# Low parts of every second up-projection weight tile by an accumulating transfer

## The chip, the cores and the metric

The kernel runs on one core of one Trainium2 chip. The metric is device time in microseconds (us) of one execution; smaller is better. A core has TensorE for matrix products (PE in the profile; PEld are its weight loads), VectorE (DVE), ScalarE (ACT), GpSimd (POOL) and SyncE (SP). Transfers from device memory (HBM) into the on-chip buffers (SBUF) are issued by SP and POOL, each in its own queue, and carried out by 16 DMA engines. Matrix products are summed up in PSUM.

## The reference, cut

Two layers over 256 tokens of width 2048, all in float32:

```
h    = rmsnorm(x) ; proj = h @ w_in[l]            # 2048 x 6144: q, k, v, gate_b, gate_c, conv_in
attn = differential attention (8 heads) of q, k, v
conv = gate_b * causal_conv3(gate_c * conv_in)
x    = x + concat([attn, conv]) @ w_out[l]        # 2048 x 2048
hm   = rmsnorm(x) @ w_up[l]                       # 2048 x 8192: the up-projection
x    = x + square(relu(hm)) @ w_down[l]           # 8192 x 2048: the down-projection
```

## The kernel before, in words

**Two parts for every operand.** To keep float32 accuracy on TensorE, each weight and each activation is split in two: a high part, which is the value rounded to the type float32r, and a low part, the value minus the high part. A product is then three products: high x high, high x low, low x high (`TERMS`, L35).

**Weight tiles.** All weights come through one stream of 768 tiles of 128 x 1024 values (512 KB), in the fixed order of the list `plan` (L269 to L285). Tiles of `w_in` for q, k, v, of `w_out` and of `w_down` cover 2 row blocks x 512 columns (`straight`); tiles of the gates, the convolution and `w_up` cover 4 row blocks x 256 columns (`turned`). `load_weights` (L288) lets SP load the next tile into one of `RAW` = 4 raw buffers. `split_weights` (L298) makes the parts: ACT copies the raw tile, rounding, into a high tile `whi` (L307), and DVE subtracts it from the raw tile into a low tile `wlo` (L308). `whi` and `wlo` have 3 buffers each (the pool `wpool`, L108). `weights` (L313) is called when TensorE's program comes to tile i; it sees to it that tiles up to i + `AHEAD` = i + 2 have been split ahead of it in program order. A buffer comes free when its last reader is done: a raw buffer after the subtraction, a high or low buffer after the matmuls that use it.

**The products.** `linear` (L322; q, k, v, w_out and down) takes a tile in 12 matmuls, three for each row block and half of the tokens. `linear_t` (L341; gates, convolution and up) holds the weights still and first runs the eight matmuls of a tile with its high part (512 columns: high and low activations side by side), then the eight with its low part (256 columns). Four tiles fill one accumulator of an up-projection step; `hidden` (L585) then takes it out of PSUM with ACT (copy of one half, relu, square, high part) and DVE (sum of the halves, low part). In each layer the MLP runs in four groups: one up stage of 8 accumulators (32 tiles), then one down stage of 32 tiles. So there are 256 up tiles. The index of a tile in `plan` decides below what is done with it; the four tiles of an up accumulator are even, odd, even, odd.

**Order.** TensorE's order is the program's own (`manual_schedule`, L115). Side work such as normalization, transposes and attention is put between the products in small pieces (`Background`, L52). The instructions of the other engines and queues are ordered by the framework's planner before the run; each engine then works through its list in order and waits where an operand isn't ready or a buffer isn't free. POOL issues transfers only for constants and tables near the start; in the MLP it has nothing to do.

**Other buffers.** `nat` (7 buffers of the tag `wide`, L109) holds intermediate 128 x 512 tiles: of `joined` and `hidden`, of the normalizations and of attention. `tmp` (3 buffers, L110) holds the scores of a head, `s`, in attention.

Of the kernel before, what the change touches and what calls it, by code (L numbers as in the profile page):

```python
# [9 lines left out]
F32 = mybir.dt.float32  # L10
F32R = mybir.dt.float32r
AF = mybir.ActivationFunctionType
ALU = mybir.AluOpType
AX = mybir.AxisListType

P = 128
# [7 lines left out]
DFF = 4 * D  # L24
# [4 lines left out]
CH = 512  # L29
WC = 256  # L30
KG = 4
RAW = 4
AHEAD = 2

TERMS = ((0, 0), (0, 1), (1, 0))  # L35
REL = 2 * S - P - 1
# [62 lines left out]
def trunk(ctx: ExitStack, tc: tile.TileContext, x, w_in, w_out, conv_w, q_norm_g, k_norm_g,  # L99
          lambda_q1, lambda_k1, lambda_q2, lambda_k2, subln_g, attn_norm_g, mlp_norm_g,  # L100
          w_up, w_down, rel_bias, selector, out):
    nc = tc.nc
# [2 lines left out]
    xpool = ctx.enter_context(tc.tile_pool(name="xpool", bufs=1))  # L105
    apool = ctx.enter_context(tc.tile_pool(name="apool", bufs=4))
    bpool = ctx.enter_context(tc.tile_pool(name="bpool", bufs=8))
    wpool = ctx.enter_context(tc.tile_pool(name="wpool", bufs=3))  # L108
    nat = ctx.enter_context(tc.tile_pool(name="nat", bufs=7))  # L109
    tmp = ctx.enter_context(tc.tile_pool(name="tmp", bufs=3))  # L110
    small = ctx.enter_context(tc.tile_pool(name="small", bufs=4))
    dram = ctx.enter_context(tc.tile_pool(name="dram", bufs=1, space=bass.MemoryType.DRAM))
    mm = ctx.enter_context(tc.tile_pool(name="mm", bufs=2, space=PSUM))
# [155 lines left out]
    plan = []  # L269
# [16 lines left out]
    loaded, parts_of = [], []  # L286

    def load_weights():  # L288
        i = len(loaded)
        if i < len(plan):  # L290
            w, row, c, nk = plan[i]
            cols = 2 * CH // nk
            raw = wpool.tile([P, nk, cols], F32, tag="raw", name=f"raw{i}", bufs=RAW)
            nc.sync.dma_start(
                raw, w[row:row + nk * P, c:c + cols].rearrange("(k p) c -> p k c", p=P))
            loaded.append(raw)

    def split_weights():  # L298
        i = len(parts_of)
        if i < len(plan):  # L300
            while len(loaded) <= i:
                load_weights()
            nk = plan[i][3]
            hi = wpool.tile([P, nk, 2 * CH // nk], F32R, tag="hi", name=f"whi{i}")
            lo = wpool.tile([P, nk, 2 * CH // nk], F32R, tag="lo", name=f"wlo{i}")
            for c in (slice(0, 1), slice(1, nk)) if i < 2 else (slice(0, nk),):
                nc.scalar.activation(hi[:, c], loaded[i][:, c], AF.Copy)  # L307
                nc.vector.tensor_sub(lo[:, c], loaded[i][:, c], hi[:, c].bitcast(F32))  # L308
            parts_of.append((hi, lo))

    used = [0]
# [1 line left out]
    def weights(w, row, c):  # L313

        i = used[0]
        used[0] += 1
        assert plan[i][1:3] == (row, c)
        while len(parts_of) < min(len(plan), i + 1 + AHEAD):
            split_weights()
        return parts_of[i]  # L320
# [45 lines left out]
    def joined(acc, name):  # L366

        low = nat.tile([P, 2, S], F32, tag="wide", name=f"{name}l")
        nc.scalar.activation(low, acc[:, :, 1], AF.Copy)
        whole = nat.tile([P, 2, S], F32, tag="wide", name=f"{name}w")  # L370
        nc.vector.tensor_add(whole, acc[:, :, 0], low)
        return whole
# [230 lines left out]
    for l in range(DEPTH):  # L603
# [3 lines left out]
        for half in range(2):  # L607
            h0 = 4 * half
            c0 = half * CH
# [16 lines left out]
        for q in range(AW // WC):  # L626
# [4 lines left out]
            i = joined(acc, f"ci{l}{q}")  # L631
# [66 lines left out]
```

## Time and profile before

| what | value |
|---|---|
| median of 3 runs | 2208.05 us (2205.59 to 2208.78) |
| the profiled execution: its own time | 2209.4 us |
| its span in the profile | 2207.6 us |
| mean granted TensorE clock | 0.999 |
| DMA packets and bytes | 302698, 410.99 MB, mean 186 GB/s |
| SP's queue, share of the 16 DMA engines | 61.0% |
| POOL's queue, share of the 16 DMA engines | 0.3% |
| read from HBM over the span | 406.96 MB |

How to read it. The profile is of one execution. In the engine rows a number in us is busy time, in brackets its share of the span, and x the count of instructions. A wait row reads: who waited, on which line, for whom, then us in total, times, the longest. A group row reads: line, engine, operation, output <- inputs with their shapes, count, then busy us and mean ns of one, then the idle time just before and what ended it. A timeline row starts with start and duration in us, a row of the chain as well. A row of the stretches table gives, for one stretch of the span, its length, each engine's busy time and count, the granted clock, the mean busy share of the DMA engines and GB/s. Issue rows end with the median us from a transfer's issue to its landing; where three numbers stand, they are the least, the median and the most.

### The profile page before, as it was taken

The page shows a single profiled execution, that of the slowest core. Times are in us where ns is not written, and L with a number is a line of the kernel's source. Part 1 is how long each engine was busy: PE and PEld are TensorE (multiplying, and loading weights), DVE is VectorE, ACT ScalarE, POOL GpSimd, SP SyncE. Part 2 cuts the span into 40 slices and gives each one's busy share as a digit, 9 for nine tenths or more (in the row PEclk, how much of TensorE's full clock was granted, in tenths as well). Part 3 has the DMA queues.
Part 4 walks back from the last instruction along what each step waited for, and adds up shares of the span by engine and source line. Part 5 has one row for each costly group of instructions (what it writes and reads, how often), then busy time and mean ns, then how long its engine had stood idle before and what let it go on. Part 6 is the DMA issues. An engine that isn't in the chain of part 4 may idle for free.

```text
span 2207.6 us, 28973 instructions
## 1 busy us (share of the span) xinstructions
PE 2193.6 (99%) x11242; PEld 1863.1 (84%) x11242; DVE 1257.4 (57%) x1561; ACT 1105.3 (50%) x1492; POOL 100.3 (5%) x120
## 2 busy tenths in 40 slices
PE   8999999999999999999999999999999999999999
PEld 6888888888888888888888888888888888888887
DVE  5577655555555555555556776555555555555554
ACT  6456445554454454355445664445534544544543
POOL 3021100000000000000011211000000000000000
PEclk9999999999999999999999999999999999999999
DMA  7554666666666666666666546666666666666665
GB/s 250 172 158 148 191 183 189 187 187 191 197 186 188 199 187 186 194 194 184 186 185 179 156 153 187 186 185 189 188 191 196 187 190 197 185 189 199 186 197 162
DMA packets 302698, 410.99 MB, mean 186 GB/s; under 512 B 12931, under 2 KB 193749, under 8 KB 302560
## 3 DMA queue, kind: packets, MB, share of 16 engines
q1 hardware_dynamic: 301520, 406.90, 61.0%
q0 software_dynamic: 992, 2.22, 0.3%
q8 instruction: 88, 1.44, 0.3%
q14 instruction: 50, 0.41, 0.1%
q10 hardware_dynamic: 48, 0.02, 0.0%
HBM read 406.96 MB, written 2.12 MB: 185 GB/s over the span
## 4 chain that ended last, share of the span: by engine, by line
PE 99%; DMA 0%; POOL 0%; DVE 0%; ACT 0%; issue 0%; SPq 0%; DVEq 0%
PE up L357 32%; PE dn L335 32%; PE o L335 8%; PE q L335 4%; PE gc L357 4%; PE ci L357 4%; PE gb L357 4%; PE k L335 4%; PE v L335 4%; PE sc L487 1%; PE av L523 1%; PE tpn L399 1%; DMA raw<-in_w_in_dram 0%; PE ptp L513 0%; PE atp L549 0%; POOL q_r L379 0%
## 5 line engine op out<-in xcount | busy, mean ns | idle before, releaser
L308 DVE TENSOR_TENSOR wlo<-raw,whi 128x1024 fp32r<-128x1024 f32 (+1 forms) x770 | 944.0, 1226 | 835.1 <-ACT whi L307 831.5
L307 ACT ACTIVATE whi<-raw 128x1024 fp32r<-128x1024 f32 (+1 forms) x770 | 813.3, 1056 | 991.9 <-PE dn L335 387.8
L335 PE MATMUL dn<-whi,hid 128*128 128x512 f32 x2048 | 632.7, 389 | 0.0
L357 PE MATMUL up<-nT,whi 128*128 128x512 f32 x2048 | 512.6, 392 | 0.0
L335 PEld LDWEIGHTS dn<-whi,hid 128*128 128x128 f32 x2048 | 384.4, 188 | 79.6
L357 PEld LDWEIGHTS up<-nT,whi 128*128 128x128 f32 x2048 | 368.8, 189 | 66.3
L335 PE MATMUL dn<-wlo,hid 128*128 128x512 f32 x1024 | 398.5, 389 | 0.0
L357 PEld LDWEIGHTS up<-nT,wlo 128*128 128x128 f32 x2048 | 279.3, 190 | 19.8
L357 PE MATMUL up<-nT,wlo 128*128 128x256 f32 x2048 | 285.7, 282 | 0.0
L335 PEld LDWEIGHTS dn<-wlo,hid 128*128 128x128 f32 x1024 | 192.2, 188 | 39.5
L335 PE MATMUL o<-whi,cat 128*128 128x512 f32 x512 | 159.6, 390 | 0.0
L335 PEld LDWEIGHTS o<-whi,cat 128*128 128x128 f32 x512 | 96.1, 188 | 19.8
L335 PE MATMUL o<-wlo,cat 128*128 128x512 f32 x256 | 99.6, 389 | 0.0
L335 PE MATMUL q<-whi,nT 128*128 128x512 f32 x256 | 86.0, 405 | 2.8 <-ACT nT L244 2.8
L335 PE MATMUL k<-whi,nT 128*128 128x512 f32 x256 | 86.6, 405 | 0.0
L335 PE MATMUL v<-whi,nT 128*128 128x512 f32 x256 | 83.4, 396 | 0.0
L357 PE MATMUL gc<-nT,whi 128*128 128x512 f32 x256 | 65.8, 396 | 0.0
L357 PE MATMUL ci<-nT,whi 128*128 128x512 f32 x256 | 65.3, 396 | 0.0
L357 PE MATMUL gb<-nT,whi 128*128 128x512 f32 x256 | 64.1, 392 | 0.0
L335 PEld LDWEIGHTS q<-whi,nT 128*128 128x128 f32 x256 | 48.9, 191 | 14.6 <-ACT nT L244 3.2
L335 PEld LDWEIGHTS k<-whi,nT 128*128 128x128 f32 x256 | 48.9, 191 | 11.0
L335 PEld LDWEIGHTS o<-wlo,cat 128*128 128x128 f32 x256 | 48.1, 188 | 9.7
(645 smaller groups left out, 1580.5 us busy)
## 6 DMA issues: line engine op xcount, KB each, us to landing
raw<-in_w_up_dram SPq DMA_DIRECT2D x256, 512.0 KB, 3.7
raw<-in_w_down_dram SPq DMA_DIRECT2D x256, 512.0 KB, 3.7
raw<-in_w_in_dram SPq DMA_DIRECT2D x192, 512.0 KB, 4.0
raw<-in_w_out_dram SPq DMA_DIRECT2D x64, 512.0 KB, 3.7
rev<-by_dist_d POOLq DMA_DIRECT2D x2, 1024.0 KB, 11.6
out_dram<-x SPq DMA_DIRECT2D x8, 256.0 KB, 3.9
x<-in_x_dram SPq DMA_DIRECT2D x3, 512.0 KB, 9.5
x<-in_x_dram SPq DMA_DIRECT2D x2, 256.0 KB, 3.8
```

The costliest lines, as they stand in the source:

```text
L307: nc.scalar.activation(hi[:, c], loaded[i][:, c], AF.Copy)
L308: nc.vector.tensor_sub(lo[:, c], loaded[i][:, c], hi[:, c].bitcast(F32))
L335: nc.tensor.matmul(acc[:, t], a.ap[:, pa, k % KG, t * P:(t + 1) * P], (hi, lo)[pw][:, j], start=(k == 0 and n == 0), stop=(k == nk - 1 and ...
L357: nc.tensor.matmul(acc[:, f, 0] if part else acc[:, f], wt[:, k % 4, fs], a.ap[:, 0, k % KG] if part else a.ap[:, :, k % KG], start=(part ...
L399: nc.tensor.transpose(tp[:, i * S + t * P:i * S + (t + 1) * P], xs[n][:, t, k * P:(k + 1) * P], ident)
L487: nc.tensor.matmul(sc[:, :W], qT[m * DK:(m + 1) * DK, a, i, t * P:(t + 1) * P], kT[m * DK:(m + 1) * DK, b, i, :W], start=(n == 0), stop=(n ...
L523: nc.tensor.matmul(av[:, i * P:(i + 1) * P], pT[:, a, k * P:(k + 1) * P], v[:, b, k, i * P:(i + 1) * P], start=(k == 0 and n == 0), stop=( ...
```

## The change

Every tile of `w_up` with an odd index in `plan` (128 of the 256) gets its low part in another way. ACT writes the negated high part into the low tile, and POOL then issues a transfer that reads the raw weights a second time from HBM and adds them to what stands in the low tile: -high + weight = low. The subtraction on DVE isn't done for these tiles, and their raw buffer is free after the high part. All other tiles are split as before. Tiles are split three ahead instead of two; `whi` and `wlo` have 4 buffers instead of 3, and in turn the raw tiles have 3 instead of 4, `wide` 6 instead of 7, and the scores 2 instead of 3.

```diff
-RAW = 4
-AHEAD = 2
+RAW = 3
+AHEAD = 3
...
-    wpool = ctx.enter_context(tc.tile_pool(name="wpool", bufs=3))
-    nat = ctx.enter_context(tc.tile_pool(name="nat", bufs=7))
-    tmp = ctx.enter_context(tc.tile_pool(name="tmp", bufs=3))
+    wpool = ctx.enter_context(tc.tile_pool(name="wpool", bufs=4))
+    nat = ctx.enter_context(tc.tile_pool(name="nat", bufs=6))
+    tmp = ctx.enter_context(tc.tile_pool(name="tmp", bufs=2))
...
             nk = plan[i][3]
             hi = wpool.tile([P, nk, 2 * CH // nk], F32R, tag="hi", name=f"whi{i}")
             lo = wpool.tile([P, nk, 2 * CH // nk], F32R, tag="lo", name=f"wlo{i}")
+            w, row, c0, _ = plan[i]
+            summed = w.shape[1] == DFF and i % 2 == 1
             for c in (slice(0, 1), slice(1, nk)) if i < 2 else (slice(0, nk),):
                 nc.scalar.activation(hi[:, c], loaded[i][:, c], AF.Copy)
-                nc.vector.tensor_sub(lo[:, c], loaded[i][:, c], hi[:, c].bitcast(F32))
+                if not summed:
+                    nc.vector.tensor_sub(lo[:, c], loaded[i][:, c], hi[:, c].bitcast(F32))
+            if summed:
+
+                nc.scalar.activation(lo, hi.bitcast(F32), AF.Copy, scale=-1.0)
+                cols = 2 * CH // nk
+                nc.gpsimd.dma_start(
+                    lo, w[row:row + nk * P, c0:c0 + cols].rearrange("(k p) c -> p k c", p=P),
+                    accum_op=ALU.add)
             parts_of.append((hi, lo))
```

## The prediction

> **What bounds the kernel now.** I read the page first, then what TensorE waits for.
>
> ```profile
> span 2207.6 us, 28973 instructions
> PE 2193.6 (99%) x11242; PEld 1863.1 (84%) x11242; DVE 1257.4 (57%) x1561; ACT 1105.3 (50%) x1492; POOL 100.3 (5%) x120
> ...
> PE 99%; DMA 0%; POOL 0%; DVE 0%; ACT 0%; issue 0%; SPq 0%; DVEq 0%
> ```
> ```profile
> PE gps L151 <- POOL ident masks.py:199: 3.6, 1, 3.6
> PE q L335 <- ACT nT L244: 2.8, 1, 2.8
> PE q00tp L465 <- DVE q00n L456: 2.4, 1, 2.4
> PE tpn L399 <- DMA x<-in_x_dram: 0.6, 1, 0.6
> ```
>
> The chain is TensorE alone, and the second fence is the whole list of its waits. It idles 2207.6 - 2193.6 = 14.0 us in all, in the first 50 us. No wait on a weight tile is in that list. Less work on DVE therefore buys nothing directly: even with every idle microsecond gone the kernel would gain 0.6%. The question is only whether the change makes TensorE wait.
>
> The place is the up-projection. The chain in order of time, then the stretches table, then the timeline inside one stage:
>
> ```profile
> 580.51 89.36 PE up L357 x512
> 669.87 87.07 PE dn L335 x384
> ```
> ```profile
> core 0: us, PE busy (x) PEld busy (x) DVE busy (x) ACT busy (x) POOL busy (x), PEclk, DMA share, GB/s
> 580.50:669.90 89.40, 89.40 (x514) 78.70 (x513) 49.57 (x48) 50.06 (x61) 0.00 (x0) 1.00 0.63 189
> 669.90:756.90 87.00, 87.00 (x385) 72.01 (x384) 44.42 (x40) 35.28 (x36) 0.00 (x0) 1.00 0.63 193
> ```
> ```profile
> 599.87 2.00 PE L357 MATMUL up<-nT,whi 128*128 128x512 f32 x8
> 601.71 1.11 PE L357 MATMUL up<-nT,wlo 128*128 128x256 f32 x8
> 602.66 2.00 PE L357 MATMUL up<-nT,whi 128*128 128x512 f32 x8
> ...
> 601.91 1.06 ACT L307 ACTIVATE whi<-raw 128x1024 fp32r<-128x1024 f32 x1 [1.73 <-PE up L357]
> 602.88 0.59 ACT L369 ACTIVATE h011l<-up 128x512 f32<-128x512 f32 x1
> 604.70 1.06 ACT L307 ACTIVATE whi<-raw 128x1024 fp32r<-128x1024 f32 x1 [1.24 <-PE up L357]
> 605.67 0.61 ACT L589 ACTIVATE h011w<-h011w 128x512 f32<-128x512 f32 x1
> 606.32 0.64 ACT L590 ACTIVATE h011s<-h011w 128x512 f32<-128x512 f32 x1
> 606.98 0.63 ACT L575 ACTIVATE hid<-h011s 128x512 fp32r<-128x512 f32 x1
> ```
>
> An up stage takes 89.4 us for 32 tiles, so 2.79 us a tile and 11.17 us for the four tiles of one accumulator. There are 8 such stages: 256 tiles, 64 groups of four, 715 us. Within a tile the eight high matmuls take 1.84 us (601.71 - 599.87) and the eight low ones 0.95 us (602.66 - 601.71). Each ACT high part starts 0.2 us after the high matmuls that free its buffer (601.91 against 601.71). The DMA engines are already 0.63 busy with the weights. The change adds to this resource.
>
> **DVE and ACT.** The prices are the group rows of the split:
>
> ```profile
> L308 DVE TENSOR_TENSOR wlo<-raw,whi 128x1024 fp32r<-128x1024 f32 x766 | 941.5, 1229 | 830.9 <-ACT whi L307 827.3 <-PE up L357 2.4
> L307 ACT ACTIVATE whi<-raw 128x1024 fp32r<-128x1024 f32 x766 | 811.0, 1059 | 986.7 <-PE dn L335 387.8 <-PE up L357 302.2 <-PE o L335 83.5
> ```
>
> DVE loses 128 subtractions, 128 x 1.23 = 157 us, all beside matmuls: worth 0. ACT gains 128 negated copies of the same shape as the high part, so 1.06 us each, 136 us. In a stage ACT goes from 50.1 to 50.1 + 16 x 1.06 = 67 of 89.4 us. That fits, and its cover is the spare quarter of the stage. The negation waits in ACT's queue until the low buffer four tiles back is free; behind it stand the next high part and the copy, relu, square and high part of the hidden tile (the four rows above, 2.5 us).
>
> **POOL and the accumulating transfer.** POOL does nothing in this stage now (0.00 above), so its queue is passed by nothing. The trace has no accumulating transfer, so I bound it. Nearest are the two 1 MB loads that POOL issues near the start, for the queue, and the raw loads, for size and source:
>
> ```profile
> raw<-in_w_up_dram SPq DMA_DIRECT2D x256, 512.0 KB, 3.7
> ...
> by_dist_d<-by_dist POOLq DMA_DIRECT2D x1, 23.9 KB, 1.9
> ```
> ```profile
> 29.29 1.81 POOL L208 DMA_DIRECT2D rev<-by_dist_d  x2 [1.66 <-DMA by_dist_d<-by_dist]
> ```
> ```profile
> DMA to landing us min/median/max: 10.0/11.6/13.2
> ```
> ```profile
> raw<-in_w_in_dram SPq DMA_DIRECT2D x5, 512.0 KB, 7.6
> ```
> ```profile
> 34.00:36.00 2.00, 2.00 (x10) 1.67 (x9) 1.54 (x4) 1.06 (x1) 0.39 (x1) 1.00 1.04 332
> 36.00:38.00 2.00, 2.00 (x10) 1.64 (x9) 1.56 (x2) 0.00 (x0) 0.35 (x1) 1.00 1.00 374
> 38.00:40.00 2.00, 2.00 (x11) 1.64 (x10) 0.96 (x2) 1.94 (x3) 0.63 (x3) 1.00 1.02 356
> 40.00:42.00 2.00, 2.00 (x11) 1.65 (x10) 0.95 (x1) 0.21 (x1) 2.00 (x1) 1.00 1.02 366
> ```
>
> The third fence is the landing time of those two 1 MB loads, the fourth the raw loads issued between 28 and 46 us. Read together: a raw load lands after 3.7 us when the engines are 0.63 busy, and after 7.6 us beside the two POOL loads, when the engines are full at a mean of (332 + 374 + 356 + 366) / 4 = 357 GB/s. Issuing costs POOL 0.9 us each, 16 x 0.9 = 14 of 89.4 us in a stage, and lies in the landing time.
>
> Load on the engines, by group of four tiles: four raw loads cost 0.63 x 11.17 = 7.0 us, 1.76 each. Two accumulating transfers cost at least 3.5 us if each is as cheap as a raw load: 10.6 of 11.17, share 0.94, and they fit. An accumulating transfer must also read the old contents of its target. If that read costs the engines as much as the other, they need 7.0 us: 14.1 of 11.17, and each group is 2.9 us longer, 64 x 2.9 = +186 us. Counted as bytes at the full rate instead, it is 8 x 0.524 MB / 357 GB/s = 11.75 us a group, +0.58, 64 x 0.58 = +37 us. So throughput alone says between 0 and +186; both ends stay.
>
> The Trainium skill, Collectives: The Full Stack, section "The bandwidth ceiling", says that a transfer which adds reads two sources on the same ring and moves at half the rate of a copy. By that rule alone the sum is the +186 us; no row of this case shows an addition, so it stands as a direction only.
>
> Latency is the second limit, and decides first. With four buffers, the low buffer of tile X serves tile X+4, and both are odd. The loop is: low matmuls of X (0.95), release (0.2), negation (1.06), then POOL's issue to landing (L), then the low matmuls of X+4. Four tiles last 11.17 us, so L may be 11.17 - 2.21 = 8.96 us; each microsecond beyond costs 64 us in all. L's ends: 3.7 (a raw load of this size today) and 13.2 (the slower 1 MB load). With the engines at 0.94 or more the saturated rows are nearer, 7.6 for 512 KB and 10.0 to 13.2 for 1 MB from POOL. A 512 KB addition has 1 MB to read and comes from POOL, with two in flight most of the time, as there; I take the faster of the two, 10.0, since only half of its bytes come from memory. The group then lasts 2.21 + 10.0 = 12.2 us: 64 x 1.04 = +67 us. At 7.6 it is 0, at 13.2 it is 64 x 4.24 = +271 us. A gain is excluded: TensorE waits for no tile here.
>
> **Buffers.** Three raw buffers instead of four: a raw load lasts from issue to landing, then a high part (1.06) and, for the tiles with a subtraction, 1.23. Today that is 3.7 + 2.3 = 6.0 of the 8.4 us that three tiles last: free. With landings of 7.6 it is 7.6 + 1.06 + 0.6 (half the tiles subtract) = 9.3, and 0.3 us a tile x 256 = +77 us: the same size as the loop above and in parallel, so it isn't added. At the start the fourth raw load must wait for tile 0.
>
> ```profile
> 9.67 27.97 SPq L294 DMA_DIRECT2D raw<-in_w_in_dram  x10
> ```
> ```profile
> 9.25 4.96 PE q L335 x12
> ...
> 38.02 10.07 PE k L335 x44
> ```
>
> SP now blocks at the fifth load until 9.67, when the first buffer is free; the fourth will block until then. It lands some 4 us later and is split by 16; the first product's eight tiles last from 9.25 to 38.0, so the fourth is wanted at about 20. Cost 0; without that cover, about 4 us.
>
> The wide and attention buffers (7 to 6, 3 to 2) serve steps whose only wait on the path is the 2.4 us of q00tp; in attention TensorE is busy throughout:
>
> ```profile
> 140.00:200.00 60.00, 60.00 (x355) 50.88 (x354) 45.01 (x117) 37.98 (x90) 11.79 (x16) 1.00 0.49 149
> ```
>
> Bound: one such wait in each of the four query steps, 4 x 2.4 = 10 us; below nothing is excluded by the same row. I take 0. The third tile ahead is what the latency loop already uses; elsewhere it removes no wait.
>
> **Sum.** 0 (DVE) + 0 (ACT) + 67 (landing) + 0 (buffers) on the profiled run's 2209.4 us, 1.35 us above the median of 2208.05: 2208 + 67 = 2275 us, 3.0% slower.
>
> **The rivals.** *It is hidden: no change.* The transfer lands within 8.96 us, and TensorE never sees it. For it: the full-rate rows are loads from memory, and the old contents come from SBUF. Memory would be read at 189 x 1.5 = 284 GB/s, under the 357 of those rows. An L of 3.7 to 8.9 then gives 2204 to 2212 us (the buffers' terms included); it decides the sign exactly at 8.96. Against it: a POOL transfer took 10.0 at best, and the share would be 0.94 in the cheapest case. The Trainium skill, DMA: Bandwidth & Descriptors, "Specifications", likewise puts the limit for memory reads below that of the SBUF side; no run here shows an SBUF read. Chance 0.25.
>
> *ACT is late.* The negation is queued behind the hidden tile's chain, so "three ahead" isn't reached: up to 2.5 us go off the 8.96, leaving 6.46. Then even the 7.6 stalls, 64 x 1.14 = +73, and 10.0 gives 64 x 3.54 = +227. For: the four ACT rows stand between two high parts. Against: ACT has 22 us free in a stage. 2281 to 2435 us, chance 0.08.
>
> *Additions are several times slower than copies*, worked off one by one. With three times a raw load's engine time a group needs 7.0 + 10.6 = 17.6 us, 64 x 6.4 = +410 us: 2618. Nothing in this trace speaks for or against it. Chance 0.08.
>
> *Faster.* Some of the 14.0 us of idle goes because tiles are ready earlier. But none of the four waits is on a weight's low part. 2200, chance 0.03.
>
> **How the numbers follow.** The forecast (landings of 9 to 13.2 us, or full engines) has 0.56, by itself 2212 to 2479 us. A measurement of this kernel tells 0.2% (4.4 us) from no change. Slower: 0.56 + 0.08 + 0.08 = 0.72; same 0.25; faster 0.03. The range runs from the hidden case's 2204 to 2208 + 271 = 2479 and leaves out the very slow and the faster case, about 0.11, and a few in a hundred of the late-ACT one's worst sums.
>
> **What would show it.** Right: in an up stage, waits of up's low matmuls on the accumulating transfer; the stage at about 98 us instead of 89.4, the down stage unchanged at 87; share over 0.9; landings at about 10 us on POOL's queue; raw landings at 5 to 8. The loop is right if stage time grows by 8 us for each microsecond over 8.96. Wrong: landings below 8.9 and no such wait (hidden); waits of the high matmuls on ACT, or the transfer landing in time but issued late (ACT); waits outside the up stages (the buffers).

## The result, and the profile after

The changed kernel takes 2236.26 us (median of 4 runs, 2229.01 to 2236.69) against 2208.24 (2205.59 to 2208.78): ratio 1.0122, 95% interval 1.0099 to 1.0144. It is slower by 28 us; the forecast was +67. The profiled execution is the fastest of the four, 2229.01 us with a span of 2227.2, so the profile accounts for 19.6 us of span; that the other three took 7 us more has no profile and stays open.

First the page of the changed kernel, then TensorE's waits and those of its weight loads (PEld), then the landings of the accumulating transfers.

```profile
span 2227.2 us, 29372 instructions
...
PE 2199.8 (99%) x11242; PEld 1860.2 (84%) x11242; DVE 1105.1 (50%) x1433; ACT 1223.4 (55%) x1620; POOL 266.9 (12%) x248
...
q1 hardware_dynamic: 301520, 406.90, 57.2%
q0 software_dynamic: 68576, 69.34, 19.9%
...
raw<-in_w_up_dram SPq DMA_DIRECT2D x256, 512.0 KB, 5.8
```
```profile
PE up L367 <- DMA wlo<-in_w_up_dram: 12.4, 17, 1.5
```
```profile
PEld up L367 <- DMA wlo<-in_w_up_dram: 24.4, 33, 2.0
```
```profile
DMA to landing us min/median/max: 6.2/7.4/9.5
```

Busy shares look much as before: DVE gave up 152 us, and TensorE is still 99% busy. The new lines are the two waits. Before, TensorE waited for no weight tile; now the weight loads of up's low parts wait 33 times, 24.4 us in all. The transfers behind them land after 7.4 us, not 10.0, and the raw loads after 5.8 instead of 3.7.

Where the time lies shows in the chain: the starts and lengths of the last four down stages. An up stage lasts from the end of one to the start of the next.

```profile
1599.15 87.07 PE dn L345 x384
...
1777.48 87.08 PE dn L345 x384
...
1956.62 87.07 PE dn L345 x384
...
2135.52 87.08 PE dn L345 x384
```

1777.48 - 1686.22 = 91.3, then 92.1 and 91.8 us, where each was 89.4; the down stages are unchanged. Eight stages with some 2.4 us more each are the 19.6 us. The stretches table of one up stage:

```profile
1864.60:1956.60 92.00, 90.16 (x513) 78.28 (x512) 31.64 (x33) 63.82 (x76) 19.27 (x15) 1.00 1.12 274
```

The last two columns are the share of the DMA engines and GB/s. The share is above 1, so times of packets overlap and are counted more than once; the share isn't a capacity. And one late transfer, piece by piece, in the chain of the changed kernel:

```profile
1717.42 1.24 DVE wlo L311
1718.66 0.02 issue
1718.68 7.10 DMA raw<-in_w_up_dram
...
1725.86 1.07 ACT whi L309
...
1726.95 1.07 ACT wlo L314
1728.02 0.28 issue
1728.31 8.80 DMA wlo<-in_w_up_dram
1737.11 0.04 issue
1737.15 22.96 PE up L367 x131
```

Read from below: TensorE goes on at 1737.15, when a transfer of 8.80 us has landed. It was issued at 1728.31, behind a negation that started only at 1726.95, because its high part waited for a raw load of 7.10 us, and that load for a subtraction to free one of the three raw buffers. The low matmuls four tiles back had started at 1724.51:

```profile
1724.51 1.19 PE L367 MATMUL up<-nT,wlo 128*128 128x256 f32 x8
```

From there to 1737.15 is 12.64 us, where four tiles take 11.17. The forecast's loop is there, with 8.80 for the landing. But 1.3 us of it is a negation that came late (1726.95 against 1724.51 + 0.95 + 0.2 = 1725.66).

This one is typical of the trace. Only two of the 128 landings pass 8.96 us (9.2 and 9.5). Of the 33 tiles whose weight loads waited, 27 have a high part that started within 0.1 us of the landing of its raw load, and in 10 a copy of the hidden tile stands between the high part and the negation, for another 0.35 us. ACT's waits on raw loads in all:

```profile
ACT whi L309 <- DMA raw<-in_w_up_dram: 149.4, 96, 2.8
```

### The profile page after: what moved, and what is told of

Its sections match the earlier page's. It is cut to its first block, busy times and chain, and to the rows that moved or that the text cites. A ratio compares the mean times of both kernels' runs of the same rounds, so it can differ in the third digit from the quotient of the medians.

```text
span 2227.2 us, 29372 instructions
## 1 busy us (share of the span) xinstructions
PE 2199.8 (99%) x11242; PEld 1860.2 (84%) x11242; DVE 1105.1 (50%) x1433; ACT 1223.4 (55%) x1620; POOL 266.9 (12%) x248
## 3 DMA queue, kind: packets, MB, share of 16 engines
q0 software_dynamic: 68576, 69.34, 19.9%
## 4 chain that ended last, share of the span: by engine, by line
PE 80%; DMA 12%; ACT 4%; issue 2%; DVE 1%; POOL 0%; DVEq 0%; ACTq 0%; POOLq 0%
PE dn L345 31%; PE up L367 16%; PE o L345 8%; DMA raw<-in_w_up_dram 6%; DMA wlo<-in_w_up_dram 5%; PE gc L367 4%; PE ci L367 4%; PE gb L367 4%; PE v L345 4%; PE k L345 4%; PE q L345 3%; ACT whi L309 2%; DVE wlo L311 1%; ACT wlo L314 1%; PE sc L497 1%
## 5 line engine op out<-in xcount | busy, mean ns | idle before, releaser
L311 DVE TENSOR_TENSOR wlo<-raw,whi 128x1024 fp32r<-128x1024 f32 (+1 forms) x642 | 787.6, 1227 | 890.3 <-ACT whi L309 887.1
L316 POOL DMA_DIRECT2D wlo<-in_w_up_dram x128 | 164.6, 1286 | 1325.1 <-ACT wlo L314 1240.3
L367 PEld LDWEIGHTS up<-nT,wlo 128*128 128x128 f32 x2048 | 276.4, 190 | 41.8 <-DMA wlo<-in_w_up_dram 24.4
L314 ACT ACTIVATE wlo<-whi 128x1024 fp32r<-128x1024 f32 x128 | 135.1, 1056 | 2.2
```

The costliest lines, as they stand in the source:

```text
L314: nc.scalar.activation(lo, hi.bitcast(F32), AF.Copy, scale=-1.0)
L316: nc.gpsimd.dma_start(lo, w[row:row + nk * P, c0:c0 + cols].rearrange("(k p) c -> p k c", p=P), accum_op=ALU.add)
L367: nc.tensor.matmul(acc[:, f, 0] if part else acc[:, f], wt[:, k % 4, fs], a.ap[:, 0, k % KG] if part else a.ap[:, :, k % KG], start=(part ...
```

## The experiments

Theory A: the forecast's latency loop, with the landing alone against its 8.96 us. Theory B: late raw loads delay the negation inside that loop. Theory C: ACT's queue does. Rivals: the new buffer counts cost by themselves; the engines are full, so that slack doesn't help. Each result stands beside runs of the kernel before on the same chip (2208.5 to 2208.9 us there). The changed kernel wasn't run again beside them; one of its four times is 7 us under the other three, so what a mend gave back of the 28 us is known to some 7 us only. Profiles are therefore compared with profiles as well: from the first matmul of each up stage to the first of its down stage, the eight up stages took 716.6 us in the profile before and 735.8 in that of the changed kernel, 19.2 more.

**The buffers without the second transfer.**

```diff
-            summed = w.shape[1] == DFF and i % 2 == 1
+            summed = False
```

> The new buffer counts and tiles made three ahead, with all low parts by subtraction on DVE as before (no second transfer). Theories A, B and C: the up stages last 89.4 us again, 2204 to 2212 us. Rival (the smaller raw, wide and score buffers cost by themselves): over 2214.

2210.39 us against 2208.91, ratio 1.0004 (0.9995 to 1.0014). The buffer counts cost nothing that can be told, as long as there is no second transfer.

**A plain transfer in place of the addition.**

```diff
-                    lo, w[row:row + nk * P, c0:c0 + cols].rearrange("(k p) c -> p k c", p=P),
-                    accum_op=ALU.add)
+                    lo, w[row:row + nk * P, c0:c0 + cols].rearrange("(k p) c -> p k c", p=P))
```

> The changed kernel with the accumulating transfer made a plain one of the same size from the same queue; it overwrites the negated part, so the low part is the raw weight and the subtraction is left out. All theories: 2207 to 2214 us if the second read of the addition is what it costs, the transfer's landing falling from 7.4 to about 5 us and its share of engine time to that of a raw load (3.4 us to about 1.7 us each). If a landing near 7 us stays, the queue of POOL is the cost and not the addition, and the time stays at 2228 to 2238.

2208.77 us against 2208.91, ratio 1.0000 (0.9990 to 1.0009). Its page, its landings and an up stage:

```profile
q0 software_dynamic: 68576, 69.34, 12.6%
```
```profile
DMA to landing us min/median/max: 4.2/5.0/6.5
```
```profile
1850.50:1939.80 89.30, 89.30 (x513) 78.62 (x512) 31.63 (x33) 64.17 (x76) 11.12 (x15) 1.00 0.97 281
```

The same bytes from memory, the same queue, the same negation ahead of it, and no loss: landings never pass 6.5 us. The low tile then holds the weight itself; the sum is left out. The whole 28 us hangs on the addition. It makes a landing 2.4 us longer, and by the queue's share its packets take (19.9 - 0.3)% of 2227.2 us / 128 = 3.4 us of the 16 engines against (12.6 - 0.3)% of 2207.9 / 128 = 2.1, where 1.7 was expected; the 0.3% are the constants.

**Four raw buffers.**

```diff
-RAW = 3
+RAW = 4
...
-    nat = ctx.enter_context(tc.tile_pool(name="nat", bufs=6))
+    nat = ctx.enter_context(tc.tile_pool(name="nat", bufs=4))
```

> The changed kernel with four raw buffers instead of three; the room comes from the wide tiles (4 instead of 6). In the changed profile the accumulating transfers land after 7.4 us (median), below the 8.96 us that the loop of the prediction allows, and 96 high parts in the up stages wait for a raw load, 149 us in all. Theory A (the landing alone closes the loop, 2.2 us + landings of up to 9.5): a fourth raw buffer doesn't help, 2228 to 2240 us, as many waits on the transfer. Theory B (three raw buffers with landings near 6 us make the high part late by 1 to 2.5 us, and with it the negation, so that the transfer is issued late): the waits on raw loads and on the transfer mostly go, 2207 to 2214 us. Theory C (the copy of the hidden tile stands ahead of the negation in ACT's queue): about half of the loss stays, 2218 to 2228.

2223.48 us against 2208.91, ratio 1.0071 (1.0056 to 1.0087): by the medians half of the loss went, by the profiles 5 of 19 us (up stages of 730.9 us). No high part in the up stages waits for a raw load any more (in the changed kernel 96 did). What is left shows in TensorE's weight loads and in this kernel's timeline, ACT and then POOL:

```profile
PEld up L367 <- DMA wlo<-in_w_up_dram: 18.9, 29, 1.4
```
```profile
1715.74 0.58 ACT L379 ACTIVATE h112l<-up 128x512 f32<-128x512 f32 x1
1716.22 1.05 ACT L314 ACTIVATE wlo<-whi 128x1024 fp32r<-128x1024 f32 x1
```
```profile
1717.57 1.28 POOL L316 DMA_DIRECT2D wlo<-in_w_up_dram  x1 [4.65 <-PE up L367]
```
```profile
DMA to landing us min/median/max: 6.2/7.7/9.7
```

The hidden tile's copy stands ahead of the negation, and landings reach 9.7. The time lies in theory C's range. Theory A's refusal of any gain fell, and theory B was right in part: the waits on raw loads went, but weight loads still wait for a transfer 29 times, 18.9 us, where it was 33 times, 24.4 us, and now 14 landings pass 8.96 us. One tile on which neither a raw load nor a copy is late, from the low matmuls of X to those of X+4:

```profile
1708.99 1.11 PE L367 MATMUL up<-nT,wlo 128*128 128x256 f32 x8
...
1709.19 1.06 ACT L309 ACTIVATE whi<-raw 128x1024 fp32r<-128x1024 f32 x1 [0.44 <-PE up L367]
1710.28 1.06 ACT L314 ACTIVATE wlo<-whi 128x1024 fp32r<-128x1024 f32 x1
...
1711.63 1.28 POOL L316 DMA_DIRECT2D wlo<-in_w_up_dram  x1 [3.81 <-ACT wlo L314]
...
1720.64 1.21 PE L367 MATMUL up<-nT,wlo 128*128 128x256 f32 x8 [0.32 <-DMA wlo<-in_w_up_dram]
```

The negation doesn't start when the low buffer is free (0.95 + 0.2 = 1.15 us after the low matmuls' start) but behind its own high part, which waited for X's high matmuls to free the high buffer: 0.20 + 1.06 + 0.03 = 1.29. And 0.29 us pass from its end (1711.34) to the issue, which the forecast's loop hasn't got. 1720.64 - 1708.99 = 11.65 us are 0.48 more than 11.17.

**The negation on DVE.**

```diff
-                nc.scalar.activation(lo, hi.bitcast(F32), AF.Copy, scale=-1.0)
+                nc.vector.tensor_scalar_mul(lo, hi.bitcast(F32), -1.0)
```

> The changed kernel with the negated copy made by DVE instead of ACT; three raw buffers as there. Theory A (landing loop): the loop only trades one copy for another, 2228 to 2240 us. Theory B (raw buffers): raw loads are still late, but the negation can start right behind the high part, 2220 to 2236. Theory C (ACT's queue): the 0.6 us copy ahead of every second negation is out of the way and ACT has room, 2208 to 2218.

2218.94 us against 2208.91, ratio 1.0043 (1.0028 to 1.0058): by the medians 17 of the 28 us went, by the profiles 8 of 19 (up stages of 727.8 us). That is between the ranges of theories C and B. The group row of the negation:

```profile
L314 DVE TENSOR_SCALAR wlo<-whi 128x1024 fp32r<-128x1024 f32 x128 | 88.8, 693 | 172.1 <-ACT whi L309 172.1
```

It takes 0.69 us on DVE, 1.06 on ACT, and no copy of ACT's stands ahead of it. The two savings weren't parted. Raw loads still come late here (70 waits, 104.6 us).

**Both.** The two diffs above together.

> Both mends together: four raw buffers (wide 4) and the negated copy on DVE. Alone they gave back about half each (2223.5 and 2218.9 us of the changed kernel's 2236.3, against 2208.9 before). Theories B and C together (late raw loads and ACT's queue eat the slack of the loop, and the landing alone fits): no wait is left but those of landings over 9 us, 2208 to 2214. Theory A (landings alone): the waits on the transfer stay, 2217 or more.

2220.40 us against 2208.69, ratio 1.0056 (1.0039 to 1.0072). By the medians that is no better than the negation on DVE alone, and theories B and C together missed: some 11 us stay. By the profiles the savings nearly add up: 5 and 8 us alone, 12 of 19 together (up stages of 723.6 us). With one profile of each kernel this isn't settled. The landings and the weight loads' waits:

```profile
DMA to landing us min/median/max: 6.4/7.5/10.3
```
```profile
PEld up L367 <- DMA wlo<-in_w_up_dram: 9.0, 13, 1.4
```

The 13 waits left come with landings of 7.4 to 10.3 us, all in the first 30 us of an up stage; in this kernel's chain one lands 22 us into a stage:

```profile
1855.02 11.28 PE up L367 x64
...
1867.38 10.28 DMA wlo<-in_w_up_dram
1877.70 68.27 PE up L367 x392
```

Why these land late wasn't tried.

**Every fourth tile.**

```diff
-            summed = w.shape[1] == DFF and i % 2 == 1
+            summed = w.shape[1] == DFF and i % 4 == 1
```

> The changed kernel with every fourth up tile made by the accumulating transfer instead of every second (64 instead of 128), the others by subtraction. All theories of a loop that is only just exceeded: landings fall under 7 us with half of the traffic and the loss goes, 2207 to 2212 us. A fixed price for each transfer (on POOL or in the queue) would leave half of the loss, 2219 to 2225.

2215.55 us against 2208.69, ratio 1.0030 (1.0019 to 1.0041): a quarter of the loss for half of the transfers. That is over the 2212 of the loop theories and under the 2219 of a fixed price. Landings are 6.7 us in the median and again up to 9.5; eight weight loads waited, 6.0 us.

**Every tile.**

```diff
-            summed = w.shape[1] == DFF and i % 2 == 1
+            summed = w.shape[1] == DFF
```

> The changed kernel with every up tile made by the accumulating transfer (256). A group of four tiles moves 8 tiles from memory and reads 4 more in SBUF. If the second read takes as much of the engines as one from memory: 12 x 0.524 MB at 357 GB/s = 17.6 us a group instead of 11.17, 64 x 6.4 = +412, 2550 to 2640 us. If only the bytes from memory count: 8 x 0.524 / 357 = 11.75 us, 2230 to 2290 us, with the latency loop on top.

2620.67 us against 2208.69, ratio 1.1864 (1.1846 to 1.1882), as expected of full engines on which the second read counts like the first. The raw loads, an up stage, and the landings:

```profile
raw<-in_w_up_dram SPq DMA_DIRECT2D x256, 512.0 KB, 12.0
```
```profile
858.00:996.00 138.00, 94.62 (x498) 73.69 (x498) 13.54 (x19) 77.35 (x89) 38.23 (x30) 1.00 1.17 240
```
```profile
DMA to landing us min/median/max: 9.0/14.3/15.9
```

The table shows 240 GB/s; with the four reads in SBUF beside eight from memory that is 240 x 12 / 8 = 360, close to the 357 of the full engines in the profile before. The raw loads of the other queue land after 12.0 us as well, and single additions land 2.4 us apart where the mean is 17.6 / 4 = 4.4, so it isn't POOL's queue alone that is full.

**Two ahead, with the old buffers.**

```diff
-RAW = 3
-AHEAD = 3
+RAW = 4
+AHEAD = 2
...
-    wpool = ctx.enter_context(tc.tile_pool(name="wpool", bufs=4))
-    nat = ctx.enter_context(tc.tile_pool(name="nat", bufs=6))
-    tmp = ctx.enter_context(tc.tile_pool(name="tmp", bufs=2))
+    wpool = ctx.enter_context(tc.tile_pool(name="wpool", bufs=3))
+    nat = ctx.enter_context(tc.tile_pool(name="nat", bufs=7))
+    tmp = ctx.enter_context(tc.tile_pool(name="tmp", bufs=3))
```

> The accumulating transfers with all buffers and the two tiles ahead of the kernel before (raw 4, high and low 3, wide 7, scores 3). With three low buffers the transfer of tile X+3 has from the end of tile X's low matmuls to 2 x 2.79 + 1.84 us later, less release and negation (1.3) and 0.3 to issue: a landing of at most 5.9 us. Measured landings are 6.2 to 9.5. Loop theory: each of the 128 is late by 0.3 to 1.5 us, 2245 to 2400 us, with a wait at nearly every one. If the third tile ahead didn't matter, 2220 to 2240 as in the changed kernel.

2320.52 us against 2208.69, ratio 1.0505 (1.0482 to 1.0529).

```profile
PEld up L367 <- DMA wlo<-in_w_up_dram: 117.9, 107, 3.7
```
```profile
DMA to landing us min/median/max: 5.9/6.7/9.4
```

The loop's arithmetic holds: 112 us over 128 transfers is 0.87 us each, and a median landing of 6.7 is 0.8 over the 5.9 that fit. The third tile ahead, with its buffers, is worth 84 us to this change.

**Four ahead.**

```diff
-AHEAD = 3
+AHEAD = 4
...
-    wpool = ctx.enter_context(tc.tile_pool(name="wpool", bufs=4))
-    nat = ctx.enter_context(tc.tile_pool(name="nat", bufs=6))
-    tmp = ctx.enter_context(tc.tile_pool(name="tmp", bufs=2))
+    wpool = ctx.enter_context(tc.tile_pool(name="wpool", bufs=5))
+    nat = ctx.enter_context(tc.tile_pool(name="nat", bufs=4))
+    tmp = ctx.enter_context(tc.tile_pool(name="tmp", bufs=1))
...
-            p = tmp.tile([P, S], F32, tag="p", name=f"p{h}_{t}", bufs=2)
+            p = tmp.tile([P, S], F32, tag="p", name=f"p{h}_{t}", bufs=1)
...
-            pT = tmp.tile([P, 2, S], F32R, tag="pT", name=f"pT{h}_{t}", bufs=2)
+            pT = tmp.tile([P, 2, S], F32R, tag="pT", name=f"pT{h}_{t}", bufs=1)
```

> The changed kernel with tiles made four ahead and five high and low buffers (three raw buffers as there). The room comes from wide tiles (4), scores and their transposes (1 each), which may slow attention, so the up stages are read for themselves. The low buffer then has 2.79 us more: a landing of up to 11.7 us fits. Latency loop (a landing, made longer by late raw loads and ACT's queue, against 8.96 us): the up stages go back from about 91.5 to 89.4-89.7 us, no waits on the transfer. Full engines (8 tile-sized reads a group, 4.19 MB at 357 GB/s = 11.75 us): the up stages stay at 91 us or more, the waits move to the raw loads.

2230.53 us against 2208.49, ratio 1.0098 (1.0081 to 1.0115); the whole isn't comparable, since attention waits for its few buffers: the first down stage starts at 503.1 us, in the changed kernel at 494.3. The up stages by the chain, and TensorE's weight loads:

```profile
503.12 87.07 PE dn L345 x384
...
680.25 87.07 PE dn L345 x384
...
857.68 87.07 PE dn L345 x384
...
1606.26 87.07 PE dn L345 x384
...
1782.94 87.07 PE dn L345 x384
```
```profile
PEld up L367 <- DMA wlo<-in_w_up_dram: 4.8, 6, 1.3
```

680.25 - 590.19 = 90.1, then 90.4 and 89.6 us: 0.7 over the 89.4 of before in the mean, where the changed kernel was 2.4 over. Over all eight up stages, counted as above, it is 720.5 us, 3.9 over the kernel before where the changed kernel was 19.2 over. With 2.79 us more slack and the same traffic over 70% of the loss is gone, and waits of 24.4 us are 4.8. So most of it was latency. The 0.5 to 0.7 us a stage that stay are over the expected 0.3.

**The negation three times, on DVE.**

```diff
-                nc.vector.tensor_scalar_mul(lo, hi.bitcast(F32), -1.0)
+                for _ in range(3):
+                    nc.vector.tensor_scalar_mul(lo, hi.bitcast(F32), -1.0)
```

> The kernel with the negated copy on DVE (2218.9 us), the copy made three times, one behind the other, so that each transfer is issued 1.4 us later with the same traffic. Latency loop: landings of 7.4 us (median) meet 9.3 - 1.4 = 7.9 us less what late raw loads take, so half or more of the transfers come late by about 1 us: 2235 to 2275 us. Full engines: the traffic is the same and the copies are hidden, 2215 to 2224 us.

2340.14 us against 2208.49, ratio 1.0592 (1.0577 to 1.0608): 121 us above the single negation with the same traffic. Full engines as the only cause are out. The size was missed: 1.9 us a group for 1.4 us of delay. In this kernel's timeline the hidden tile's sum also stands between the copies of a tile, another 0.68:

```profile
1804.82 0.69 DVE L315 TENSOR_SCALAR wlo<-whi 128x1024 fp32r<-128x1024 f32 x1 [1.57 <-ACT whi L309]
1805.43 0.68 DVE L382 TENSOR_TENSOR h113w<-up,h113l 128x512 f32<-128x512 f32 x1
1806.03 1.41 DVE L315 TENSOR_SCALAR wlo<-whi 128x1024 fp32r<-128x1024 f32 x2
```

## Why the prediction was right or wrong, point by point

**Bound and place: right.** (Of the 14.0 us idle before, 4.7 lie behind the last matmul and 2.4 at 51 us, not in the first 50; nothing hangs on it.) TensorE waits for nothing else than before but up's low parts; DVE's 152 us bought nothing, and the down stages kept their 87.1 us.

**The landing: wrong in size; the term that failed.** The forecast put L at 10.0, "the faster of the two" 1 MB loads, for +67. Measured: 7.4 in the median, 6.2 to 9.5. By the forecast's own formula the median would have cost 0, and of the 128 landings only two would have cost anything. The other pieces of the loop were too small as well. It runs through the high part, as the timeline with four raw buffers shows: 1.29 + 1.06 + 0.29 and 0.04 behind the landing are 2.68 us, not 2.21, so a landing of 8.5 fits, not 8.96; 12 of the 128 pass that. The row it leaned on moves twice the bytes into SBUF; the addition's second read adds only 2.4 us to the 5.0 of a plain load of its size. And one value for L was the wrong tool so near to what fits: loops stall singly, when a long landing and a late negation meet.

**Raw buffers: wrong.** The forecast had the raw ring "the same size as the loop above and in parallel, so it isn't added". It is in series: a late raw load makes the high part late, and so the negation, inside the loop. The fourth buffer alone gave back 13 of 28 us by the medians, 5 of 19 by the profiles. The forecast had also looked at raw landings of 7.6; 5.8 was enough.

**ACT: partly wrong.** Its time was hidden as forecast, but its queue wasn't: the rival "ACT is late" was given 0.08, and moving the negation off ACT gave back 17 of 28 us by the medians, 8 of 19 by the profiles, a faster copy and a clear queue together. So the forecast's single term is at least three: a landing's spread, raw loads, ACT. By the medians both mends together gave back no more than one, by the profiles nearly the sum of the two, so how large each share is stays open.

**The loop and the price of a microsecond: right in form.** 11.17 us a group is the measure: with one tile less ahead 112 us, with one more the waits all but go, and a negation prolonged costs more than expected, not less.

**Throughput: the byte end was right, the share end wrong.** The +186 rested on shares that add up to at most 1; they went to 1.12. In bytes with the second read, the changed kernel moves 274 x 8 / 6 = 365 GB/s in an up stage, inside the 332 to 374 of the forecast's rows of full engines. So the engines are nearly full, which lengthens landings; they aren't the bound that more slack can't pass, as four ahead shows. The Trainium skill, Collectives: The Full Stack, "The bandwidth ceiling", says of the reduction in a collective that its add needs two source reads on the same ring and so gets half of a copy's rate. It isn't about a transfer like this one, but with every tile added the trace agrees that both reads count: 360 GB/s with the second read, 240 without. Beside half as many additions the price of one was less than double: packet time 3.4 to 2.1 us, landing 7.4 to 5.0.

**Hidden: refuted, though close.** Its reason was that a read in SBUF takes nothing from the path to memory, with the Trainium skill's DMA: Bandwidth & Descriptors, "Specifications", beside it. In the kernel with every tile added, memory was read at 240 GB/s only, while with a plain transfer on every second tile it was read at 281: the SBUF read has its price on the engines, whatever the limit at memory.

**Buffers elsewhere, start, three ahead: right**, at 1.0004 for the buffers alone.

**Open:** the 7 us between the profiled run and the others; what makes single landings of 8 to 10 us, which keep 7 us even with half of the transfers and 11 with both mends; and the shares of raw loads, ACT and landings in the 28 us.

## What to carry to other kernels

Work moved to a transfer was paid in latency here, before the DMA engines were the limit: write down the loop from one use of the buffer to the next, with every queue that the operand passes, and compare it with the time between uses, for long landings and not for the median. A wait on an earlier load in that loop is in series with it, even when the load has its own ring of buffers. An engine with half of its time free isn't worth relieving when another one bounds the kernel.

## What the runs showed that wasn't expected

Beside the share of 1.12: issuing an accumulating transfer keeps POOL for 1.29 us, a plain one of the same size and rows 0.74 (groups of 128, 164.6 and 95.3 us):

```profile
L316 POOL DMA_DIRECT2D wlo<-in_w_up_dram x128 | 164.6, 1286 | 1325.1 <-ACT wlo L314 1240.3 <-PE up L367 60.7 <-DMA wlo<-in_w_up_dram 9.9
```
```profile
L316 POOL DMA_DIRECT2D wlo<-in_w_up_dram x128 | 95.3, 744 | 1377.1 <-ACT wlo L314 1204.3 <-DMA wlo<-in_w_up_dram 82.6 <-PE up L366 80.0
```

The first row is of the changed kernel, the second of the one with plain transfers.
